# Attention scores and transposed weights in one pool of five PSUM banks

## The chip, the cores and the metric

The kernel runs on one core of one Trainium2 chip. The metric is the device time of one execution in microseconds, as the median of several runs. Engines are called by the profile's names: PE is TensorE (PEld its weight loads), DVE is VectorE, ACT is ScalarE, POOL is GpSimd, SP is SyncE, which here issues the DMAs.

## The reference, cut to what matters

One step of a hybrid decoder layer: 16 meta tokens and 2048 prompt tokens (width 1024), and 8 single-token decode rows with 4096 cached keys each. Token mixing is stick-breaking attention (8 heads of 64) beside a pooling mixer; a gated ConvFFN (2816 wide) follows. The change touches the prompt's attention:

```
def stick_breaking(q, k, v, q_pos, k_pos, sb_bias):
    z = jnp.einsum('bqhd,bkhd->bhqk', q, k) * ATTN_SCALE + sb_bias
    valid = k_pos[None, :] < q_pos[:, None]
    neg = jnp.where(valid, -jax.nn.softplus(z), 0.0)
    suffix = lax.cumsum(neg, axis=3, reverse=True) - neg
    a = jnp.where(valid, jnp.exp(jax.nn.log_sigmoid(z) + suffix), 0.0)
    return jnp.einsum('bhqk,bkhd->bqhd', a, v)
...
h = rmsnorm(xp, norm_mix_g)
q, k, v, u = project_mix(h, w_in)
xp = xp + jnp.concatenate([o_attn, o_pool], axis=-1) @ w_out
f, conv_prompt = conv_ffn(rmsnorm(xp, norm_ffn_g), zero_prefix, w_up, conv_w, conv_b, w_down)
```

The product over later keys is taken as a running product of 1 - sigmoid(z), from the newest key to the oldest.

## The kernel before

All matrices are float32. A product is made of three matmuls on split operands (`mm3`, lines 166 to 168): high x high, high x low, low x high.

**Attention and projections (the first 1180 us or so).** The eight heads are taken as four pairs (`hp`). For each pair, the query blocks (16 meta rows, then 16 blocks of 128 rows) are crossed with chunks of up to 512 keys; a query block and a chunk are one *unit*, 45 for each pair and 180 in all. `chain` does the first half of a unit, for both heads of the pair: the scores `z` (two matmuls into one PSUM bank, L518), two sigmoids on ACT that read that bank (`om` = 1 - sigmoid at L519, `be` = sigmoid at L520), a scan along the keys on DVE (L527 for the newest chunk, L529 for the others), and the product of `be` with the shifted scan (L534, in turn on POOL and DVE). POOL's memset at L513 sets the last column of `om`. `turn` does the second half: PE transposes the weights `be`, four 128x128 blocks to a PSUM tile `tt` (L572) and a small tile `ttm` for the meta keys (L582), and ACT or DVE copies them to SBUF (`at`, `atm`, L565; the diagonal block is masked on the way by DVE, L561). `weigh` takes two units at a time: both are turned, and then their products with the values run in one go (`po`, L615). The first half of a unit runs up to five units ahead of its second half (`LAG`).

Between units, `fill_to` issues other work in small pieces: the transposes of the normalised input (`turned`, `tpx`), the input projections q, k, v, u (`project`, PSUM tile `psm`), the transposes of keys and values for the outputs (`put_tok`, `pk`), the small rows (`few_rows`), the folded pooling weights (`fold_pool`, `pkf` and `pkw`). During the last pair of heads, each finished query block is projected by `w_out` (`out_tile`, PSUM tile `pso`, in psm's pool).

**PSUM.** The eight banks are shared out in four pools at lines 185 to 188: `ps_mm`, two banks, for `psm` and `pso`; `ps_z`, two banks, for `z`; `ps_t`, three banks, for everything that is transposed and for small products (all with the tag `tt`; `tt_tile` hands them out); `ps_o`, one bank, for `po`. A bank is free again when the last instruction that reads its tile is done. SBUF buffers of a unit: `om` has 3, `be` 6, `at` 6 (`OMB`, `BEB`, `ATB`).

**The order.** The framework builds the program with `schedule_with_timeline_sim=True`: it runs through the kernel's instructions with modelled durations, and gives each engine a fixed order. An instruction is placed when its operands are there and its tile has a buffer, and earlier ones in the program come first. So the number of buffers has a say in the order of every engine. On the chip each engine then works its list off in order.

**Behind it.** From about 1180 us on run the ConvFFN's up projection (`psu`) with the decode rows beside it, and the down projection (`psd`). They use other PSUM pools, opened when these are closed.

Of the kernel before, what the change touches and what calls it, by code (L numbers as in the profile page):

```python
# [9 lines left out]
F32 = mybir.dt.float32  # L10
# [6 lines left out]
PSUM = bass.MemoryType.PSUM  # L17
DRAM = bass.MemoryType.DRAM

P = 128  # L20
# [28 lines left out]
CW = 512  # L49
# [12 lines left out]
def hymba_kernel(  # L62
# [109 lines left out]
    main = ctx.enter_context(ExitStack())  # L172
# [10 lines left out]
        nc.gpsimd.affine_select(out=seen[:, 1, e, :], in_=seen[:, 1, e, :], compare_op=ALU.is_gt, fill=0.0,  # L183
                                base=0, pattern=[[1, P]], channel_multiplier=-1)
    psm = main.enter_context(tc.tile_pool(name="ps_mm", bufs=2, space=PSUM, reuse_waits="tile"))
    psz = main.enter_context(tc.tile_pool(name="ps_z", bufs=2, space=PSUM, reuse_waits="tile"))
    pst = main.enter_context(tc.tile_pool(name="ps_t", bufs=3, space=PSUM, reuse_waits="tile"))
    psd = main.enter_context(tc.tile_pool(name="ps_o", bufs=1, space=PSUM, reuse_waits="tile"))
    inp = main.enter_context(ExitStack())
    pa = inp.enter_context(tc.tile_pool(name="pa", bufs=1, side="right", reuse_waits="tile"))  # L190
# [253 lines left out]
    def key_lo(j):  # L444
        return 0 if j == 0 else META + P * (j - 1)

    def attention(hp):
# [55 lines left out]
        def chain(bi, c, top, low):  # L503
            q0, M = (0, META) if bi < 0 else (META + P * bi, P)
            g = bi // 2 if bi >= 0 else -1
            if top:
                st["prev"] = None
            o = q0 - (META + QW * g if g >= 0 else 0)
            qs = slice(o, o + M)
            n = min(key_lo(4 * c + 4), key_lo(bi + 2)) - key_lo(4 * c)  # L510
            be = pb.tile([P, 2, CW], F32, name="be", bufs=BEB)
            om = pb.tile([P, 2, CW + 1], F32, name="om", bufs=OMB)
            nc.gpsimd.memset(om[:M, :, n:n + 1], 1.0)  # L513
            for e in range(2):
                h = 2 * hp + e
                z = psz.tile([P, CW], F32, name="z")
                for k in range(2):
                    nc.tensor.matmul(z[:M, :n], qs_[g, e][k][:, qs], kst[c, e][:, 0:n], start=k == 0, stop=k == 1)  # L518
                nc.scalar.activation(out=om[:M, e, 0:n], in_=z[:M, :n], func=AF.Sigmoid, scale=-SCALE, bias=nbias[:M, h:h + 1])  # L519
                nc.scalar.activation(out=be[:M, e, 0:n], in_=z[:M, :n], func=AF.Sigmoid, scale=SCALE, bias=bias[:M, h:h + 1])  # L520
                if bi < 0:
                    nc.gpsimd.affine_select(out=be[:M, e, 0:M], in_=be[:M, e, 0:M], compare_op=ALU.is_gt,
                                            fill=0.0, base=0, pattern=[[-1, M]], channel_multiplier=1)
                rv = om[:M, e, 0:n + 1][:, ::-1]
                if top:
                    hide = unseen[:M, CW - n:CW + 1] if bi >= 0 else unseen[:M, CW - P:CW - P + n + 1]
                    nc.vector.tensor_tensor_scan(out=rv, data0=rv, data1=hide[:, ::-1], initial=1.0, op0=ALU.mult, op1=ALU.max)  # L527
                else:
                    nc.vector.tensor_tensor_scan(out=rv, data0=rv, data1=zero[:M, 0:1].broadcast_to([M, n + 1]),  # L529
                                                 initial=st["prev"][:M, e, 0:1], op0=ALU.mult, op1=ALU.add)  # L530
                m0 = META if low else 0
                if n > m0:
                    cnt["mul"] += 1
                    (nc.gpsimd if cnt["mul"] % 2 == 0 else nc.vector).tensor_tensor(  # L534
                        out=be[:M, e, m0:n], in0=be[:M, e, m0:n], in1=om[:M, e, m0 + 1:n + 1], op=ALU.mult)
            bm = None
            if low:
                bm = pb.tile([P, 2, META], F32, name="bm", bufs=BEB)
                nc.vector.tensor_tensor(out=bm[:M], in0=be[:M, :, 0:META], in1=om[:M, :, 1:META + 1], op=ALU.mult)
            st["prev"] = om  # L540
            return be, bm

        def turn(ab, bi, c, top, low):
# [54 lines left out]
            return prods, copies, (end if low else None)  # L598

        return units, fetch, chain, turn  # L600

    pob = psd.tile([P, 4, P], F32, name="po")
# [167 lines left out]
    pst = ctx.enter_context(tc.tile_pool(name="pu_t", bufs=1, space=PSUM, reuse_waits="tile"))  # L770
# [482 lines left out]
```

## Time and profile before

| | us |
|---|---|
| median of 3 runs | 2768.55 (2767.65 to 2773.09) |
| profiled execution | 2771.54 |
| its span | 2769.8 |
| PE busy | 2662.7 |
| DVE busy | 1805.2 |
| ACT busy | 1031.4 |

The span is what the profile covers; the views below divide this span. "Busy" of PE counts pipelined matmuls that overlap, so a busy PE need not be at its peak. A wait is named "who waits, at which line, for whom", and is put down to the semaphore that came last by the profile. Where POOL's product at L534 is waited for, the view may name the memset at L513, the next POOL instruction.

### The profile page before, as it was taken

How to read it: one execution, taken by the hardware profiler on the slowest of the kernel's cores; microseconds unless marked ns; L12 is line 12 of the kernel's file. 1: busy time of each engine (PE TensorE's matmuls, PEld its weight loads, DVE VectorE, ACT ScalarE, POOL GpSimd, SP SyncE). 2: the span in 40 equal slices, each digit the busy share in tenths (PEclk: the TensorE clock that was granted, in tenths of full speed). 3: DMA queues.
4: the chain of work that ended last, by engine and by line, in shares of the span. 5: the costliest groups of instructions: out<-in, count | busy, mean ns of one | idle time of the engine just before them, and what ended most of it. 6: DMA issues, size and time to landing. Idle time of an engine off the chain costs nothing.

```text
span 2769.8 us, 39760 instructions
## 1 busy us (share of the span) xinstructions
PE 2662.7 (96%) x14759; PEld 2089.6 (75%) x14759; DVE 1805.2 (65%) x3037; ACT 1031.4 (37%) x1833; POOL 721.7 (26%) x736
## 2 busy tenths in 40 slices
PE   5899999999998999999999999999999999999998
PEld 4677777787786888778877777777776777777776
DVE  4588768857669588669977777777774541114434
ACT  4466656655557256423322222222222320012111
POOL 0012212211122011145554554445554200000000
PEclk9899999999999999999999999999999999999999
DMA  7653552454425433455556555646656574666551
GB/s 252 218 178 118 167 179 97 130 203 136 165 87 171 159 117 101 147 193 193 184 208 242 207 201 213 227 165 237 215 206 237 173 258 165 200 205 212 179 194 64
DMA packets 326375, 498.79 MB, mean 180 GB/s; under 512 B 25367, under 2 KB 238631, under 8 KB 309781
## 3 DMA queue, kind: packets, MB, share of 16 engines
q1 hardware_dynamic: 307749, 362.03, 39.8%
q0 software_dynamic: 18432, 134.23, 12.7%
q8 instruction: 116, 1.90, 0.3%
q14 instruction: 78, 0.64, 0.1%
HBM read 395.99 MB, written 100.59 MB: 179 GB/s over the span
## 4 chain that ended last, share of the span: by engine, by line
PE 79%; DVE 3%; issue 2%; DMA 2%; ACT 1%; POOL 0%; SPq 0%; DVEq 0%; ACTq 0%; POOLq 0%
PE psu L166 12%; PE psu L167 12%; PE psu L168 12%; PE psd L166 6%; PE psd L168 6%; PE psd L167 6%; PE po L615 4%; PE z L518 3%; PE tt L572 3%; PE dav L950 2%; PE psm L166 2%; PE psm L168 2%; PE psm L167 2%; PE pso L167 2%; PE pso L166 2%; PE pso L168 2%
## 5 line engine op out<-in xcount | busy, mean ns | idle before, releaser
L166 PE MATMUL psu<-h2c,uwh 128*128 128x512 f32 x1408 | 555.0, 394 | 4.0 <-ACT uwh L160 2.2
L168 PE MATMUL psu<-h2c,uwl 128*128 128x512 f32 x1408 | 550.7, 391 | 1.3 <-DVE uwl L161 1.3
L167 PE MATMUL psu<-h2c,uwh 128*128 128x512 f32 x1408 | 551.6, 392 | 0.0
L534 POOL TENSOR_TENSOR be<-be,om 128x512 f32<-128x512 f32 (+3 forms) x176 | 182.6, 1037 | 844.2 <-DVE om L529 302.0
L1048 DVE SCALAR_TENSOR_TENSOR cv<-psu,par,cv 128x511 f32<-128x511 f32 x352 | 261.2, 742 | 146.5 <-ACT cv L1045 142.9
L166 PEld LDWEIGHTS psu<-h2c,uwh 128*128 128x128 f32 x1408 | 265.2, 188 | 81.1 <-issue 10.9
L1059 POOL TENSOR_TENSOR cv<-cv,cv 128x512 f32<-128x512 f32 x88 | 224.7, 2554 | 388.6 <-DVE cv L1053 290.7
L168 PEld LDWEIGHTS psu<-h2c,uwl 128*128 128x128 f32 x1408 | 265.3, 188 | 63.7 <-issue 7.3
L167 PEld LDWEIGHTS psu<-h2c,uwh 128*128 128x128 f32 x1408 | 265.3, 188 | 62.1 <-issue 8.5
L529 DVE TENSOR_TENSOR_SCAN om<-om,zero 128x513 f32<-128x513 f32 (+1 forms) x224 | 274.0, 1227 | 46.2 <-ACT om L519 41.2
L519 ACT ACTIVATE om<-z,nbias 128x512 f32<-128x512 f32 (+5 forms) x360 | 213.3, 593 | 138.3 <-PE z L518 83.4
L1045 ACT ACTIVATE cv<-psu,par 128x512 f32<-128x512 f32 x176 | 136.4, 776 | 289.1 <-PE psu L168 289.1
L1220 DVE TENSOR_TENSOR xt<-psd,xt 128x512 f32<-128x512 f32 x64 | 44.0, 691 | 281.8 <-PE psd L168 281.7
L520 ACT ACTIVATE be<-z,bias 128x512 f32<-128x512 f32 (+5 forms) x360 | 211.4, 589 | 0.6 <-PE tt L572 0.6
L167 PE MATMUL psm<-hk,wh 128*128 128x512 f32 x512 | 206.6, 404 | 2.9 <-DVE hk L226 2.9
L166 PE MATMUL psm<-hk,wh 128*128 128x512 f32 x512 | 205.0, 406 | 1.9 <-ACT hk L225 1.3
L168 PE MATMUL psm<-hk,wl 128*128 128x512 f32 x512 | 204.2, 399 | 1.0 <-DVE wl L161 1.0
L161 DVE TENSOR_TENSOR uwl<-uwr,uwh 128x1024 fp32r<-128x1024 f32 x94 | 121.1, 1290 | 127.8 <-ACT uwh L160 127.8
L166 PE MATMUL psd<-wd,ah 128*128 128x512 f32 x512 | 200.3, 395 | 0.0
L167 PE MATMUL psd<-wd,ah 128*128 128x512 f32 x512 | 200.0, 392 | 0.0
L168 PE MATMUL psd<-wd,al 128*128 128x512 f32 x512 | 199.4, 390 | 0.0
L160 ACT CAST uwh<-uwr 128x1024 fp32r<-128x1024 f32 x94 | 98.8, 1054 | 246.4 <-PE psu L167 230.4
(245 smaller groups left out, 4773.8 us busy)
## 6 DMA issues: line engine op xcount, KB each, us to landing
hk<-hs_s SPq DMA_DIRECT2D x96, 512.0 KB
uwr<-in_w_up_dram SPq DMA_DIRECT2D x88, 512.0 KB
act_s<-sg SPq DMA_DIRECT2D x88, 256.0 KB
ar<-act_s SPq DMA_DIRECT2D x32, 704.0 KB
raw<-in_w_up_dram SPq DMA_DIRECT2D x40, 512.0 KB
xt<-in_x_prompt_dram SPq DMA_DIRECT2D x32, 512.0 KB
hs_s<-hk SPq DMA_DIRECT2D x32, 512.0 KB
uwr<-in_w_down_dram SPq DMA_DIRECT2D x22, 512.0 KB
```

Source lines behind the costliest of these rows:

```text
L161: nc.vector.tensor_tensor(out=lo, in0=src, in1=f32(hi), op=ALU.subtract)
L166: nc.tensor.matmul(ps, ah, bh, start=i == 0, stop=False)
L167: nc.tensor.matmul(ps, ah, bl, start=False, stop=False)
L168: nc.tensor.matmul(ps, al, bh, start=False, stop=i == n - 1)
L519: nc.scalar.activation(out=om[:M, e, 0:n], in_=z[:M, :n], func=AF.Sigmoid, scale=-SCALE, bias=nbias[:M, h:h + 1])
L520: nc.scalar.activation(out=be[:M, e, 0:n], in_=z[:M, :n], func=AF.Sigmoid, scale=SCALE, bias=bias[:M, h:h + 1])
L529: nc.vector.tensor_tensor_scan(out=rv, data0=rv, data1=zero[:M, 0:1].broadcast_to([M, n + 1]), initial=st["prev"][:M, e, 0:1], op0=ALU.mul ...
L534: (nc.gpsimd if cnt["mul"] % 2 == 0 else nc.vector).tensor_tensor(out=be[:M, e, m0:n], in0=be[:M, e, m0:n], in1=om[:M, e, m0 + 1:n + 1], o ...
L615: mm = nc.tensor.matmul(o, v_, a_, start=start, stop=stop, skip_group_check=True).ins
L1045: nc.scalar.activation(out=t, in_=ps, func=AF.Identity, scale=cpar(2, fi), bias=cpar(3, fi))
L1048: nc.vector.scalar_tensor_tensor(out=t[:, o:], in0=ps[:, 0:CW - o], scalar=cpar(d, fi), in1=t[:, o:], op0=ALU.mult, op1=ALU.add)
L1059: nc.gpsimd.tensor_tensor(out=cv[1], in0=cv[0], in1=cv[1], op=ALU.mult)
```

## The change

`z` is taken from the pool `ps_t` with the tag `tt`, which then has five banks; `ps_z` is gone. Both kinds of tile are one bank large. A free bank of the five can go to a score, to a transpose or to any other tile with that tag.

```
-    psz = main.enter_context(tc.tile_pool(name="ps_z", bufs=2, space=PSUM, reuse_waits="tile"))
-    pst = main.enter_context(tc.tile_pool(name="ps_t", bufs=3, space=PSUM, reuse_waits="tile"))
+    pst = main.enter_context(tc.tile_pool(name="ps_t", bufs=5, space=PSUM, reuse_waits="tile"))
...
-                z = psz.tile([P, CW], F32, name="z")
+                z = pst.tile([P, CW], F32, name="z", tag="tt")
```

## The prediction

> **What bounds the kernel now.** I read the page first: which engine is busy, and what the chain that ended last is made of.
>
> ```profile
> PE 2662.7 (96%) x14759; PEld 2089.6 (75%) x14759; DVE 1805.2 (65%) x3037; ACT 1031.4 (37%) x1833; POOL 721.7 (26%) x736
> PE 79%; DVE 3%; issue 2%; DMA 2%; ACT 1%; POOL 0%; SPq 0%; DVEq 0%; ACTq 0%; POOLq 0%
> ```
>
> TensorE (PE) is busy 96% of the span, and 79% of the chain is its own work. A change that adds or removes no instruction can only change what PE loses while it waits. So the second view is the table of stretches, cut where the pool that changes is in use: from the first attention units to the first rows of the FFN.
>
> ```profile
> 0.00:100.00 100.00, 64.76 (x348) 51.09 (x349) 47.21 (x148) 45.83 (x86) 8.31 (x58) 0.90 0.72 241
> 100.00:1182.00 1082.00, 1023.53 (x6958) 818.24 (x6957) 812.25 (x1397) 617.73 (x1281) 198.55 (x364) 0.98 0.44 147
> 400.00:500.00 100.00, 92.80 (x722) 72.89 (x718) 79.74 (x114) 63.28 (x134) 25.24 (x43) 0.97 0.22 74
> 600.00:700.00 100.00, 99.52 (x722) 79.50 (x721) 70.68 (x115) 55.59 (x118) 16.18 (x34) 1.00 0.48 160
> 800.00:870.00 70.00, 62.85 (x489) 50.58 (x489) 55.87 (x96) 48.14 (x108) 16.32 (x29) 0.98 0.39 120
> 1182.00:2769.80 1587.80, 1574.42 (x7455) 1220.30 (x7454) 945.73 (x1494) 367.88 (x467) 514.83 (x314) 1.00 0.58 199
> ```
>
> The columns are the stretch, its length, then busy time (and instructions) of PE, its weight loads, DVE, ACT and POOL, the granted clock, the DMA share and GB/s. From 1182 us on, other pools are open, and I take these 1587.8 us as fixed. The first 100 us are fixed too: DMA is at 0.72 there, and nearly no attention runs. What is left is 1082 us with 1082 - 1023.5 = 58.5 us of idle PE. Some stretches have no hole (99.52 of 100 at 600 us); others do (92.80 at 400 us, 62.85 of 70 at 800 us).
>
> The third view is the list of waits, for PE and its weight loads between 100 and 1182 us: waits in total, how many, the longest.
>
> ```profile
> PE tt L572 <- POOL om L513: 10.3, 6, 2.6
> PE z L518 <- ACT be L520: 7.8, 16, 1.6
> PE tt L572 <- DVE at L565: 4.8, 6, 1.2
> PE ttm L582 <- DVE at L561: 1.0, 1, 1.0
> PE tt L572 <- ACT at L565: 0.8, 2, 0.6
> PE tt L572 <- DVE mt L309: 0.8, 1, 0.8
> PE tt L572 <- DVE at L561: 0.5, 1, 0.5
> PE tt L572 <- ACT wf L404: 0.3, 1, 0.3
> PEld z L518 <- ACT be L520: 16.4, 28, 1.9
> PEld tt L572 <- DVE at L565: 7.2, 9, 1.5
> PEld tt L572 <- ACT at L565: 1.9, 6, 0.8
> PEld tt L572 <- DVE mt L309: 1.2, 1, 1.2
> PEld tt L572 <- DVE at L561: 1.0, 1, 1.0
> PEld tt L572 <- ACT wf L404: 0.6, 1, 0.6
> ```
>
> A score matmul z reads queries and keys and nothing that be (L520) writes. So "z waits for be" can only be the bank: that activation is the last reader of an older score. Likewise a transpose tt that waits for a copy at, mt or wf waits for that copy to empty a bank. The first row is different: there the products of POOL (L534, just before the memset that is named) are late, and no bank helps.
>
> **The change, part by part.** *Removed and added.* No matmul, copy or DMA is removed or added; banks stay eight (2 + 2 + 3 + 1 becomes 2 + 5 + 1). All work terms are 0, and no queue gets an instruction more.
>
> *Bank waits.* As idle time of PE proper they are 7.8 for scores and 4.8 + 1.0 + 0.8 + 0.8 + 0.5 + 0.3 = 8.2 for transposes, 16.0 us together. Counted at the weight loads, which stop a little earlier than the matmuls behind them, they are 16.4 + 7.2 + 1.9 + 1.2 + 1.0 + 0.6 = 28.3 us. I take 16.0, because the weight load's wait partly lies under the matmul still running, and keep 28.3 as the far end.
>
> *How much of this a shared pool ends.* For that I need how full the banks are. The next rows are the same stretch for instructions on z alone (PE, weight loads, ACT), and on tt (PE, weight loads, DVE, ACT).
>
> ```profile
> 100.00:1182.00 1082.00, 198.24 (x704) 115.52 (x704) 370.88 (x704) 0.98 0.44 147
> 100.00:1182.00 1082.00, 166.03 (x1088) 129.19 (x1088) 76.09 (x128) 95.86 (x188) 0.98 0.44 147
> ```
>
> Writing and reading scores takes 198.2 + 370.9 = 569 us out of 2 x 1082 bank-microseconds, 26%. Transposes take 166.0 + 76.1 + 95.9 = 338 of 3 x 1082, 10% (banks are also held while nobody works on them, and the projections' transposes add some). Together that is 907 of 5 x 1082, 17%. The waits come from bunching, not from a full PSUM, and one side is often empty when the other is full. I take three quarters of the 16.0 as ended: 12.0 us. All five taken at once is what remains.
>
> *What is late next.* After a bank wait PE meets the next late operand, the products of the first row (10.3 us now): they depend on scans and products of DVE, busy 79.74 of 100 us in the holed stretch at 400 us. I let a third of the 12.0 go into that, so -8.0 us.
>
> *Order.* The order on each engine is not the program's; it is planned when the kernel is built, and bank releases are an input. Here PE breaks off a running projection for a score, resumes it, and breaks it off again for the score of the other head:
>
> ```profile
> 601.54 0.39 PE L167 MATMUL psm<-hk,wh 128*128 128x512 f32 x1
> 601.78 0.28 PE L518 MATMUL z<-kst,qh 128*128 128x256 f32 x1
> 601.89 0.28 PE L518 MATMUL z<-kst,ql 128*128 128x256 f32 x1
> 602.01 0.40 PE L168 MATMUL psm<-hk,wl 128*128 128x512 f32 x1
> 602.25 0.40 PE L166 MATMUL psm<-hk,wh 128*128 128x512 f32 x1
> 602.48 0.40 PE L167 MATMUL psm<-hk,wh 128*128 128x512 f32 x1
> 602.72 0.28 PE L518 MATMUL z<-kst,qh 128*128 128x256 f32 x1
> ```
>
> With five banks scores can stand earlier and in pairs. That moves nothing off PE: 1023.5 us of work has to pass. It moves the cover, because projection work used later is there later. The trace of before can't show the new order. I bound it by the hole of one bad stretch: 100 - 92.80 = 7.2 us lost or won, and take 0.
>
> *The seam at 1182 us.* The FFN's pools open on banks of these pools. The last scores and copies free them in another order; by the longest bank wait in the rows (1.9 us) this is worth -1.9 to +1.9, and I take 0.
>
> *Sum.* The profiled execution took 2771.54 us, 1.7 more than its span of 2769.8 and 3.0 more than the median of the three runs, 2768.55. 2771.5 - 8.0 = 2763.5 there, so 2760.5 at the median, -0.29%. By the far end (28.3, all ended, nothing late behind it) it would be 2740.2; by PE's bound (nothing ended) 2768.5.
>
> **Rivals.** *Bigger gain.* If earlier scores also bring scans and products forward, the 10.3 us behind POOL goes with the bank waits: 16.0 + 10.3 = 26.3, so 2742. For it: DVE and ACT have room on average (812.25 and 617.73 of 1082). Against: in the holed stretch DVE is near 80%, and the om buffers (three) still hold a unit back. The Trainium skill (Perfetto Trace Analysis, Optimization Strategy) reads a gap that keeps coming back on the busiest engine as a possible lack of PSUM or SBUF for the next tile. By that rule up to the whole 58.5 us would be in reach, 2710; the rows name a bank for 16.0 of it.
>
> *No change.* PE has other work planned wherever a score lacks a bank, as at 601.78, and the holes at 400 and 800 us belong to DVE, whose scans and products set the pace there. Then nearly every bank wait reappears as a wait for be: -2 us, 2766.5. For it: PE has 99.52 of 100 in the stretch at 600 us.
>
> *Slower: scores sit on the transposes' banks.* Today at most two banks can be parked with scores that wait for ACT; then it can be five. A transpose that comes ready then waits until a score has passed both sigmoids:
>
> ```profile
> L519 ACT ACTIVATE om<-z,nbias 128x512 f32<-128x512 f32 x144 | 99.8, 693 | 58.5 <-PE z L518 39.3 <-issue 12.7 <-POOL om L513 2.8
> L520 ACT ACTIVATE be<-z,bias 128x512 f32<-128x512 f32 x144 | 99.0, 689 | 0.0
> 115.40 0.50 PE L167 MATMUL psm<-hk,wh 128*128 128x512 f32 x1 [2.90 <-DVE hk L226]
> 117.98 0.63 PE L167 MATMUL psm<-hk,wh 128*128 128x512 f32 x1
> ```
>
> That is 0.693 + 0.689 = 1.4 us each. Transposes come in runs for two units, 90 runs in 180 units; where a projection stands behind them on PE in program order, it too is stuck, since PE is in order. Six such runs cancel my 8.0 us (6 x 1.4 = 8.4); 14 give 19.6 - 8.0 = +11.6 us, 2780. Long waits cost more: after the 2.90 us hole in the rows a 512-column matmul soon takes 0.63 us, not 0.39 as at 601.54. The Trainium skill (TensorE: Matmul & The Clock Gate, A second HAM failure mode: psum-queue depth-cycling) tells of a kernel whose walk through the PSUM banks left short idles that cost it the clock. The trace agrees in kind, with a clock of 0.97 in the stretch at 400 us against 1.00 at 600. Against this rival: ACT is busy 57% (617.73 of 1082) and empties a score soon.
>
> *Order alone.* The plan changes and a hole opens or closes somewhere: 7.2 us either way, 2761 or 2776.
>
> **How the numbers follow.** Three runs of before lie 0.2% apart, about what this kernel's measurement can tell from no change: 5.5 us. Chances: my forecast (2752 to 2765) 0.37, of which 0.04 lies within 0.2%; bigger gain 0.08; no change 0.25; slower by parked scores 0.22; order alone 0.08 (0.03 faster, 0.02 same, 0.03 slower). Faster is 0.33 + 0.08 + 0.03 = 0.44, same 0.04 + 0.25 + 0.02 = 0.31, slower 0.22 + 0.03 = 0.25. The range for 8 in 10 reaches from 2745, almost the bigger gain, to 2781, the slower case with 14 runs; what lies outside is half of the bigger gain and a good third of the parked scores.
>
> **What would show it.** Right: PE busy above 1023.5 in a stretch that ends earlier than 1182 us, waits of z for be below 4 us and of tt for copies below 4, four score matmuls in a row more often, and the FFN's 1587.8 us unchanged. Wrong: new rows "tt waits for be L520" or "z waits for at", which are the parked banks; or the bank rows gone and the row behind POOL grown by as much; or a granted clock below 0.98 over the stretch. If the FFN part moves by more than 2 us, my view of what is fixed was wrong.

## The result and the profile after

The changed kernel takes 2799.8 us (median of 3 runs, 2798.91 to 2803.35) against 2768.55: a ratio of 1.0112, interval [1.0089, 1.0135]. It is slower by some 31 us where 8 us less were forecast, and the time lies outside the range. The profiled execution took 2799.8 us, its span is 2798.1 (before 2769.8: +28.3). Lines of the changed kernel stand one lower than before (z is now L517, the copies L560 and L564).

The page of the changed kernel, the busy times and the shares of the chain of waits:

```profile
PE 2675.8 (96%) x14759; PEld 2107.8 (75%) x14759; DVE 1814.0 (65%) x3037; ACT 1028.5 (37%) x1833; POOL 735.3 (26%) x736
PE 83%; DVE 7%; DMA 4%; issue 3%; ACT 2%; SPq 1%; POOL 0%; DVEq 0%; ACTq 0%; POOLq 0%
```

The instructions are the same 14759. PE is busy 13.1 us longer (2675.8 against 2662.7), and idle 122.3 us instead of 107.1, 15.2 more: 28.3 together. The stretches tell where, first those of the kernel before, then those of the changed one (the stretch, its length, busy time and instructions of PE, its weight loads, DVE, ACT and POOL, then granted clock, DMA share, GB/s).

```profile
100.00:300.00 200.00, 179.10 (x1274) 140.87 (x1273) 161.70 (x266) 128.43 (x264) 40.65 (x69) 0.97 0.46 156
300.00:850.00 550.00, 530.58 (x3739) 425.67 (x3739) 392.26 (x630) 321.32 (x686) 106.02 (x204) 0.99 0.44 147
850.00:1182.00 332.00, 313.86 (x1951) 251.70 (x1948) 258.29 (x503) 167.98 (x333) 51.88 (x91) 0.98 0.44 142
```

```profile
0.00:100.00 100.00, 68.13 (x350) 55.30 (x351) 40.54 (x137) 40.60 (x74) 5.10 (x52) 0.90 0.74 246
100.00:300.00 200.00, 172.29 (x1173) 136.09 (x1171) 156.51 (x262) 121.55 (x254) 42.80 (x72) 0.91 0.41 142
300.00:850.00 550.00, 527.08 (x3680) 426.64 (x3681) 390.16 (x606) 317.76 (x669) 108.34 (x196) 0.98 0.44 147
850.00:1182.00 332.00, 313.34 (x1997) 253.36 (x1996) 259.57 (x496) 167.04 (x347) 60.45 (x101) 0.96 0.40 129
100.00:1182.00 1082.00, 1012.71 (x6848) 816.10 (x6847) 806.24 (x1363) 606.35 (x1268) 211.60 (x368) 0.96 0.42 140
1210.00:2799.00 1589.00, 1574.20 (x7460) 1220.46 (x7459) 946.12 (x1489) 367.75 (x467) 514.03 (x313) 1.00 0.58 199
```

The last row is the FFN with 1574.20 us of PE work, as before (1574.42). Its first matmul comes 28.7 us later and its end 28.3 us later, so nothing is lost behind the seam. In the first 100 us DVE does 40.54 us instead of 47.21, ACT 40.60 instead of 45.83: attention work is missing there. By 300 us PE has 350 + 1173 = 1523 matmuls behind it instead of 348 + 1274 = 1622, 99 fewer, and the clock in 100 to 300 us is 0.91 instead of 0.97. Busy time times clock is an estimate of the work done at full speed. For the stretches to 100, 300, 850 and 1182 us it says +3.0, -16.9, -8.7 and -6.8 us, -29.4 in all (the clock has two digits, so some 5 us either way). By this estimate about half of the loss is made by 300 us and the other half later.

The timeline of PE shows the missing work. First the kernel before: the first six scores of 128 rows, by columns (144, 272, 400 keys), with the first of the two matmuls of each.

```profile
60.30 0.33 PE L518 MATMUL z<-kst,qh 128*128 128x144 f32 x1 [0.57 <-ACT be L520]
62.55 0.33 PE L518 MATMUL z<-kst,qh 128*128 128x144 f32 x1
62.84 0.34 PE L518 MATMUL z<-kst,qh 128*128 128x272 f32 x1
63.74 0.39 PE L518 MATMUL z<-kst,qh 128*128 128x272 f32 x1 [0.24 <-ACT be L520]
64.50 0.45 PE L518 MATMUL z<-kst,qh 128*128 128x400 f32 x1 [0.24 <-ACT be L520]
71.15 0.70 PE L518 MATMUL z<-kst,qh 128*128 128x400 f32 x1 [6.02 <-ACT qh L160]
75.62 2.77 PE L222 MATMUL tpx<-ident,xp 128*128 128x128 f32 x12
```

The same scores in the changed kernel (the sixth follows at 102.70 us):

```profile
72.52 3.67 PE L221 MATMUL tpx<-ident,xp 128*128 128x128 f32 x16 [3.49 <-DVE xp L231]
79.41 1.03 PE L221 MATMUL tpx<-ident,xp 128*128 128x128 f32 x8
82.58 1.04 PE L221 MATMUL tpx<-ident,xp 128*128 128x128 f32 x8
100.82 0.60 PE L352 MATMUL pk<-ident,kf 128*128 128x128 f32 x4
101.17 0.31 PE L517 MATMUL z<-kst,qh 128*128 128x144 f32 x1
101.44 0.28 PE L517 MATMUL z<-kst,qh 128*128 128x144 f32 x1
101.66 0.34 PE L517 MATMUL z<-kst,qh 128*128 128x272 f32 x1
101.96 0.29 PE L517 MATMUL z<-kst,qh 128*128 128x272 f32 x1
102.20 0.40 PE L517 MATMUL z<-kst,qh 128*128 128x400 f32 x1
```

Six scores that stood ahead of the transposes of the input (tpx), at 60 to 71 us, now stand behind all 32 of them and behind two more groups of pk transposes of keys (at 94.01 and 100.82 us), at 101 us. They don't wait for their operands: the last queries of the first four are split by 61.4 us, 1 us later than before, and those of the last two by 71.4 us (before 74.2). PE does more of the other work meanwhile (68.13 us by 100 us against 64.76).

The reason lies in the order that was planned when the kernel was built. In the built program of the changed kernel, PE begins the 847 tiles of the shared pool in the order in which the program asks for them, without exception, as it does the 487 and the 360 of the two pools of before, each pool for itself. The six scores above follow eight tiles of tpx (four transposes each) and two of pk in the program. In the shared pool they are therefore given no bank before these have theirs, even if one stands empty. In a pool of their own the scores may overtake. I call this taking turns.

The waits of PE for banks of this pool in the changed kernel, 100 to 1220 us:

```profile
PE z L517 <- DVE at L564: 12.0, 8, 3.1
PE z L517 <- DVE at L560: 7.9, 9, 1.8
PE z L517 <- DVE atm L564: 3.8, 2, 2.5
PE ttm L581 <- DVE at L564: 2.7, 2, 1.9
PE tt L571 <- DVE atm L564: 2.2, 2, 1.1
PE ttm L581 <- DVE at L560: 2.1, 1, 2.1
PE tt L571 <- DVE at L560: 0.8, 1, 0.8
PE z L517 <- ACT be L519: 0.6, 1, 0.6
```

"z waits for be" fell from 7.8 to 0.6, and the 10.3 us behind POOL are gone. In their place scores wait for the copies that empty a transpose's bank, 12.0 + 7.9 + 3.8 = 23.7 us. One such wait on the timeline:

```profile
284.48 1.33 DVE L533 TENSOR_TENSOR be<-be,om 128x512 f32<-128x512 f32 x1
285.74 0.68 DVE L564 COPY at<-tt 128x512 f32<-128x512 f32 x1
286.47 0.45 PE L517 MATMUL z<-kst,qh 128*128 128x400 f32 x1 [3.06 <-DVE at L564]
```

The copy stands on DVE behind two scans (2.46 us) and a product of 1.33 us, and the score starts 0.05 us after the copy ends (285.74 + 0.68).

### The profile page after: what moved, and what is told of

Same layout as the page of the kernel before. It is cut to its first block, busy times and chain, and to the rows that moved or that the text cites. A ratio compares the mean times of both kernels' runs of the same rounds, so it can differ in the third digit from the quotient of the medians.

```text
span 2798.1 us, 39728 instructions
## 1 busy us (share of the span) xinstructions
PE 2675.8 (96%) x14759; PEld 2107.8 (75%) x14759; DVE 1814.0 (65%) x3037; ACT 1028.5 (37%) x1833; POOL 735.3 (26%) x736
## 4 chain that ended last, share of the span: by engine, by line
PE 83%; DVE 7%; DMA 4%; issue 3%; ACT 2%; SPq 1%; POOL 0%; DVEq 0%; ACTq 0%; POOLq 0%
PE psu L166 12%; PE psu L167 11%; PE psu L168 11%; PE psd L166 6%; PE psd L168 6%; PE psd L167 6%; PE po L614 4%; PE psm L166 3%; PE psm L167 3%; PE psm L168 3%; PE z L517 3%; PE tt L571 3%; DVE om L528 2%; PE dav L949 2%; PE pso L166 2%
## 5 line engine op out<-in xcount | busy, mean ns | idle before, releaser
L533 POOL TENSOR_TENSOR be<-be,om 128x512 f32<-128x512 f32 (+3 forms) x176 | 195.4, 1110 | 863.6 <-DVE om L528 388.6
```

## The experiments

Theories: **A, the order**: scores and other tiles take turns, and this alone costs the time; either because scores are kept behind the attention's own transposes (A1: tt, ttm) or behind those of the input work (A2: tpx, pk, t24, tq and the like). **B, the banks on the chip**: a score inherits a bank that DVE empties late.

For A, the order can be had without the shared pool. These kernels keep the three pools of before and add bare ordering constraints, no semaphore, on PE's list: the first matmul of a tile `a` is planned behind that of tile `b`. (`got` lists the instructions in program order; how the table of pairs is read is left out here.)

```
+def in_turn(tc):
+    for a, b in pairs:
+        tc.add_manual_dep(got[a], got[b].name, mybir.DependencyInfo(
+            mybir.DependencyClass.NoSync, mybir.DependencyReason.SCHED_ONLY), reason="in turn")
```

**All in turn.** The pairs are all neighbours in the program's sequence of scores and transposed tiles.

> Two pools as before (2 banks for scores, 3 for transposes), but on PE the first matmul of every tile of either pool is ordered behind the first matmul of the tile that precedes it in the program, as one shared pool would force it. No score can wait here for a copy's bank. Theory A (what costs is the order: scores and transposes must take their turn): 2785 us or more. Theory B (what costs is the bank itself on the chip: a score waits for a late DVE copy): 2763 to 2775 us.

Measured 2862.76 us, 1.0345 [1.0328, 1.0362]. The order alone can cost more than the change did. It isn't a copy of the changed kernel: with two and three banks the turns may bind harder than with five.

**Scores in turn.** Only scores are kept behind the transposes that precede them.

> As the run above, in one direction alone: a score may not start before the transposes that precede it in the program have started; transposes are free. Theory A, if the loss is the scores' lost run-ahead: nearly all of the loss, 2780 us or more. Theory B: 2763 to 2775 us.

Measured 2805.2 us, 1.013 [1.0113, 1.0147], about the loss of the changed kernel.

**Transposes in turn.** Only transposes are kept behind the scores that precede them.

> The other direction alone: a transpose may not start before the scores that precede it in the program have started; scores are free. Theory A, if transposes held back by scores cost: 2780 us or more; if not, 2766 to 2772 us. Theory B: 2763 to 2775 us.

Measured 2791.2 us, 1.0082 [1.0065, 1.0099]. This direction costs too, and gradually: 57 matmuls behind at 300 us. The two add up to more than the change lost. Either they bind harder with two and three banks than with five, or the changed kernel gets something back from its five banks; no run tells these apart.

**The copies on ACT.** The changed kernel, with theory B's copies taken off DVE.

```
-        on_act = cnt["at"] % 4
+        on_act = 1
```

> The shared pool of five, with every plain copy of transposes on ACT (one in four was on DVE); the masked diagonal copies stay on DVE. Theory B: the 12.0 + 3.8 us in which scores wait for DVE's plain copies go, and with them the clock that they cost: 2775 to 2788 us. Theory A: the order still costs, 2792 us or more.

Measured 2803.44 us, 1.012 [1.0103, 1.0137], no better than the change. The rows for L564 are gone; one row of DVE is left among the scores' waits, the masked copies of the diagonal, which stay on DVE:

```profile
PE z L517 <- DVE at L560: 15.1, 10, 3.0
```

In this kernel too the first score of 128 rows comes at 103.28 us, and by 300 us 99 matmuls are missing. So the plain copies on DVE aren't what makes the loss, unless ACT, which now does them, loses as much elsewhere. What the 15.1 us for the masked copies cost is not told by this run.

**Behind the attention's transposes (A1)** and **behind the input work (A2).** The pairs now have a score as `a`, and as `b` tt and ttm alone, or all the other transposed tiles alone.

> The two pools of before; a score may not start before the attention's own transposes (tt, ttm) that precede it in the program have started. Theory A1 (scores lose by standing behind older units' transposes): 2785 to 2805 us. Theory A2 (scores lose by standing behind the tiles of the input work, tpx, pk, t24 and the like, whose data come late): 2766 to 2775 us.

> The two pools of before; a score may not start before the input work's tiles (tpx, pk, tq, t24, pkw, pkp, pkg and the like) that precede it in the program have started; attention's own transposes don't hold it. Theory A2: 2785 to 2805 us, with the first score some 10 us later than before. Theory A1: 2766 to 2775 us.

Measured 2778.55 us, 1.0034 [1.0023, 1.0046], and 2802.25 us, 1.0106 [1.0089, 1.0123]. Order behind the input work (A2) loses 32 us against the kernel before, which took 2770.26 us beside these runs. Order behind the attention's transposes (A1) loses 8 us, a little more than A2 allowed for it. As no bank is shared in either, B has no part in these losses. The stretch from 100 to 300 us of the first and of the second:

```profile
100.00:300.00 200.00, 181.90 (x1281) 142.59 (x1280) 158.92 (x268) 128.95 (x264) 43.98 (x69) 0.96 0.47 157
100.00:300.00 200.00, 168.10 (x1131) 129.18 (x1131) 149.36 (x252) 116.71 (x244) 36.32 (x65) 0.92 0.43 143
```

**Early and late.** A2's order for the first 25 units alone, and from the 26th unit on alone.

> As the run with scores behind the input work, but for the first 25 units alone (up to about 250 us). If the loss is made at the start, where the transposes of the input wait for DMA and DVE and the clock is lost with them: 2782 us or more. If it is made all along: 2770 to 2778 us.

> The complement: the order is forced from the 26th unit on. If the loss is made at the start: 2766 to 2776 us. If it is made all along: 2785 us or more.

Measured 2798.88 us, 1.0103 [1.0087, 1.012], and 2778.62 us, 1.0028 [1.0016, 1.0039], beside 2772.66 for the kernel before. 25 of 180 units, whose scores run up to about 230 us in the kernel before, make 26 us, most of A2's loss. The others cost 6 us, just above the range expected for no loss. The rows of the early one, to 100 and to 300 us:

```profile
0.00:100.00 100.00, 63.88 (x338) 50.46 (x339) 40.94 (x137) 41.02 (x74) 5.13 (x52) 0.90 0.72 241
100.00:300.00 200.00, 165.65 (x1113) 127.32 (x1112) 146.93 (x249) 114.91 (x241) 36.10 (x65) 0.94 0.43 145
```

and of the late one:

```profile
0.00:100.00 100.00, 65.50 (x350) 51.69 (x351) 47.19 (x149) 46.36 (x87) 8.32 (x58) 0.90 0.72 241
100.00:300.00 200.00, 177.30 (x1272) 139.54 (x1271) 159.56 (x264) 127.75 (x262) 40.46 (x69) 0.97 0.48 156
```

DVE's 40.94 us of the early one is the changed kernel's 40.54, and the late one's 47.19 that of before. By 300 us the early one is 1622 - 338 - 1113 = 171 matmuls behind, the late one none. In the first 100 us the early one's PE shows the same picture as the changed kernel's, though no other tile can take its two score banks:

```profile
75.14 1.94 PE L240 MATMUL tpx<-ident,xp 128*128 128x128 f32 x8 [9.07 <-DVE xp L250]
103.15 0.60 PE L371 MATMUL pk<-ident,kf 128*128 128x128 f32 x4
103.51 0.31 PE L536 MATMUL z<-kst,qh 128*128 128x144 f32 x1
```

PE stands 9.07 us before the first tpx, where before it did scores. This loss isn't made up. Where the forced order has ended, the scores run 23.2 us later than in the kernel before, from 294 to 364 us of its time, and the last one is 25.3 us late. The changed kernel goes another way: from 252 to 304 us its scores are only 3 to 9 us late (those of the early run 21 to 25), and the last one is 28.1 us late.

**A unit's scores ahead of its input work.** If the first scores only have to stand earlier in the program, issuing each unit's scores before that unit's portion of `fill_to` should mend the changed kernel; the second kernel makes the same move with the pools of before.

```
-        fill_to(max(want if ui else first, min(n_in, first + (n_in - first) * ui // END)))
...
+        if ui == 0:
+            fill_to(first)
...
+        fill_to(max(want, min(n_in, first + (n_in - first) * ui // END)))
```

> The shared pool of five, but in the program each unit's scores stand ahead of the input steps that are issued with that unit, no longer behind them. Theory A2 (scores lose their turn to the input work's tiles): a good part of the 30 us comes back, 2772 to 2790 us. If order in the program does not matter: 2795 us or more.

> The control: the same move in the program with the two pools of before, where scores take no turn with the input work's tiles. Theory A2: little, 2762 to 2776 us. If the move helps by itself, it is as much faster than before here as with the shared pool.

Measured 2803.73 us, 1.0118 [1.0102, 1.0135], and 2770.8 us, 0.9999 [0.9989, 1.0008]. A miss: the move gains nothing in either. With the shared pool the scores of 144 keys come at 80.19 us instead of 101.17, but those of 400 keys still at 104.38. So a first score that is 21 us earlier doesn't bring the time back; that several units would have to be moved is a guess that no run here tests. With pools of their own, scores overtake and the place in the program hardly matters.

**Other ways to share.** Five kernels move the borders between the banks that hold scores, the attention's transposes (tt, ttm) and the input work. For instance, for the first:

```
-    pst = main.enter_context(tc.tile_pool(name="ps_t", bufs=5, space=PSUM, reuse_waits="tile"))
+    psa = main.enter_context(tc.tile_pool(name="ps_a", bufs=4, space=PSUM, reuse_waits="tile"))
+    pst = main.enter_context(tc.tile_pool(name="ps_t", bufs=1, space=PSUM, reuse_waits="tile"))
...
-                z = pst.tile([P, CW], F32, name="z", tag="tt")
+                z = psa.tile([P, CW], F32, name="z", tag="tt")
```

> Scores and attention's transposes share four banks, the input work has one bank of its own. Theory A1: still slow, 2785 us or more. Theory A2: the loss of the shared pool goes, 2760 to 2775 us, unless one bank is too few for the input work.

> Nothing is shared: scores two banks, attention's transposes two, input work one. If taking turns is what costs, attention's transposes and the input work, which take turns in before too, gain by it: 2745 to 2765 us. If the number of banks is what counts (two for transposes in place of three shared), 2775 us or more.

> Scores and the attention's own transposes (tt, ttm) share three banks; the transposes of the input work (tpx, pk, t24, tq and the rest) keep two. Order theory: a score is no longer behind the input work, so the first 100 us go as in the kernel before and the loss is that of scores behind tt and ttm alone (+8.5 us measured) or less: 2772 to 2782. Rival, that sharing banks as such costs (copies that empty a score's bank late): about the changed kernel's +30, 2795 to 2805.

> The counterpart with the same bank counts: scores share three banks with the input work's transposes, tt and ttm keep two. Order theory: the loss of the changed kernel comes back, made in the first 200 us: 2792 to 2806, with the scores of 128x144 after 95 us. Rival, that sharing banks as such costs: the same as the kernel with scores on the banks of tt and ttm, within 5 us.

> Nothing shared: three banks for scores, two for all transposes. Tells whether the scores lacked a bank: if the 7.8 us of PE waits of z for be were the price, 2762 to 2768; if the transposes need their third bank (they were slower when the input work had one), 2775 to 2805.

| banks | us | ratio | first score of 144 keys, us |
|---|---|---|---|
| scores with tt 4, input 1 | 2814.0 | 1.0156 [1.0139, 1.0173] | 66.29 |
| scores 2, tt 2, input 1 | 2804.48 | 1.0123 [1.0106, 1.014] | 67.64 |
| scores with tt 3, input 2 | 2877.2 | 1.038 [1.0363, 1.0397] | 62.95 |
| scores with input 3, tt 2 | 2808.42 | 1.0133 [1.0116, 1.015] | 106.31 |
| scores 3, all transposes 2 | 2862.86 | 1.0329 [1.0312, 1.0346] | 62.09 |

The last column bears out when the first score comes: late in the one kernel where scores share with the input work, and early in the others. That kernel's loss is about the changed kernel's, 2.4 us above the range expected. But the times of the others don't follow the turns. By A2 I expected 2760 to 2775 for four banks shared with tt and got 2814.0; I expected 2772 to 2782 for three and got 2877.2. For three score banks I expected at most 2805 and got 2862.86. For two, two and one bank the case held in which the number of banks counts (2775 or more). These kernels are slow in their own ways. With one bank for the input work, that work runs late (x1136 and x1055 matmuls from 100 to 300 us in the first two kernels, against x1274 before). Where scores and tt share three banks, the row that the prediction named for parked scores appears at last, and where all transposes have two, the copies are late:

```profile
PE tt L572 <- ACT be L520: 21.9, 41, 1.0
PE tt L572 <- DVE at L561: 22.5, 13, 3.9
```

So the counts of banks matter as much as the turns (the last kernel shares nothing new and loses some 91 us), and these five can't show what sharing costs by itself. None of them, and no other kernel here, beats the kernel before.

## Why the prediction was wrong, point by point

**The step that failed is "Order", where I took 0.** It stood on my sentence under "The change" that a free bank of the five can go to any tile with that tag. It can't: banks go out in the program's order (847 of 847 tiles), and merging two pools merges two queues. I had noted that earlier instructions of the program come first and that bank releases are an input of the plan, and drew from it only that scores could stand earlier. They stand 41 us later at the start (60.30 against 101.17). My bound of 7.2 us, the hole of one bad stretch, was no bound: the order behind the input work imposed alone, with nothing shared, costs 32 us (2802.25 against 2770.26 us).

**The first 100 us were not fixed.** I took them so, since "nearly no attention runs" there. The little that ran was a lead, 6.7 us of DVE work and 5.2 us of ACT work, and it is gone. What this lead alone is worth isn't shown: the early run changes the order up to about 230 us, and the run with a first score at 80.19 us gained nothing.

**The bank waits had the wrong sign.** I took 12.0 of 16.0 us as ended. The scores' 7.8 for be did end (0.6 left), but new ones came: the eight rows above sum to 32.1 us. The row that I named for this, "z waits for at", is the one that appeared. The bank-microseconds (17% full) add up but didn't tell the outcome, because a bank that stands empty is of no use to a tile whose turn hasn't come.

**The rival "slower: scores sit on the transposes' banks"** had the right side, but about a third of the size (+11.6 us, 2780) and not the mechanism. "tt waits for be" is no row of weight in the changed kernel (0.4 us); the queue was blocked the other way, scores behind transposes, and first of all in the plan. That slower was among my cases is no credit to the reasoning. With three shared banks the rival's mechanism does occur, 21.9 us in 41 waits.

**The rival "bigger gain"** had one thing right: the 10.3 us behind POOL are gone. The waits for copies that came in their place are larger (23.7 us).

**PE's work.** I wrote that 1023.5 us of work has to pass and that the order moves nothing off PE. The number of matmuls is the same, but their time isn't: PE is busy 13.1 us longer over the whole span, at a clock of 0.91 instead of 0.97 from 100 to 300 us. Nearly half of the loss of 28.3 us has this form. The granted clock below 0.98 over the stretch (0.96) was among my signs of a wrong forecast. The Trainium skill (TensorE: Matmul & The Clock Gate, A second HAM failure mode: psum-queue depth-cycling) tells of a kernel in which short idles, left by cycling through PSUM banks, kept lowering the clock; the trace agrees in kind, but no run here separates the idles at banks from those at the start.

**The Trainium skill's rule** (Perfetto Trace Analysis, Optimization Strategy) that a recurring gap on the busiest engine may mean too little PSUM or SBUF for the next tile stood beside my rival of a bigger gain. For this kernel the measurement decides against reading it as "pool them": more banks within reach of each tile, and 31 us lost.

**Right** were the fixed FFN (from its first matmul to the end within 0.4 us) and that no engine gets an instruction more.

**Still open:** by times of the kernel before, the changed kernel's scores lag by 3 to 22 us from 154 to 329 us, by 17.2 at 837 and by 28.1 at 1132 us. The half of the loss that the estimate puts behind 300 us isn't assigned. The small losses of the late order (+6 us), of scores behind tt (+8) and of the waits for copies lie there together; no run took the waits for L560's copies away. At one place the traces show turns at work there too: the lag jumps from 4.4 to 19.9 us between two scores that follow each other. The second runs at 306.17 us in the kernel before, ahead of a tq and a pk tile. In the changed kernel it stands right behind both, as in the program:

```profile
306.17 0.50 PE L518 MATMUL z<-kst,qh 128*128 128x512 f32 x1
323.76 0.27 PE L306 MATMUL tq<-ident,sm 64*128 64x64 f32 x1
325.68 0.60 PE L352 MATMUL pk<-ident,kf 128*128 128x128 f32 x4
326.04 0.48 PE L517 MATMUL z<-kst,qh 128*128 128x512 f32 x1
```

The first row is the kernel before, the others are the changed one.

## What to carry to other kernels

Merging two pools doesn't only add their banks, it merges their queues: look in the program at what each tile would stand behind, above all at the start, where one kind of tile runs ahead of another. Here the order of 25 early units of 180 cost 26 us that weren't made up, on an engine that is busy 96%. So compare when the tiles of each kind run, one by one, before averages of the whole stretch; the first tile alone misleads, as the kernels with an early first score show. To test an order apart from the resource that brings it, impose the order alone on the old kernel.

## What was unexpected of the hardware

The loss shows as clock nearly as much as idle time: 13.1 us of longer busy time stand beside 15.2 us more of idle time over the span. From 105 to 150 us the changed kernel's granted clock is 0.81, and from 150 to 200 it is 0.89 (the first two rows). The kernel before has 0.89 and 0.97 (the last two):

```profile
105.00:150.00 45.00, 35.71 (x183) 26.27 (x184) 29.22 (x62) 24.07 (x53) 6.36 (x14) 0.81 0.69 235
150.00:200.00 50.00, 41.52 (x286) 33.23 (x285) 42.56 (x84) 28.49 (x61) 9.72 (x20) 0.89 0.32 103
105.00:150.00 45.00, 35.96 (x185) 25.85 (x184) 29.22 (x71) 26.35 (x54) 5.11 (x12) 0.89 0.70 245
150.00:200.00 50.00, 44.01 (x319) 34.99 (x318) 43.21 (x74) 29.66 (x64) 9.70 (x18) 0.97 0.42 134
```

From 150 to 200 us PE is busy 41.52 of 50 us against 44.01, 2.5 us less. That understates the difference: busy time times clock, the estimate from above, gives 37.0 against 42.7. From 105 to 150 us PE is idle nearly as long in both kernels (9.3 and 9.0 us), and yet the clock differs. So the idle share of a stretch doesn't tell its clock here, and what lowered it in the changed kernel isn't shown.
